# Expert weights behind all key scores: three engines in an order written by hand, and more of the first expert product ahead

## The chip, the core and the metric

The kernel runs on one core of a Trainium2 chip. A core has five engines, each with its own instruction queue that it works off in order: TensorE (PE in the rows, its weight loads PEld), VectorE (DVE), ScalarE (ACT), GpSimd (POOL) and SyncE (SP, which only issues DMAs). Sixteen DMA engines move data between the memories. The metric is the device time of one execution in microseconds (us).

## The reference, cut to what matters

One layer of a diffusion backbone on 512 tokens of width 1024: differential attention, a layer norm, and a PEER feed-forward with 16384 experts. The change is in the feed-forward alone.

```python
def peer_ffn(u, w_q, sub_keys, u_tab, v_tab):      # 8 heads, 128 keys per half, top 16
    ...
        q = (xb @ w_q).reshape(PEER_BLOCK, H, 2, PEER_QDIM // 2)
        s = jnp.einsum('thcd,ckd->thck', q, sub_keys).astype(F32)
        s1, i1 = lax.top_k(s[:, :, 0], KT)
        s2, i2 = lax.top_k(s[:, :, 1], KT)
        cand_s = (s1[..., :, None] + s2[..., None, :]).reshape(PEER_BLOCK, H, KT * KT)
        cand_i = (i1[..., :, None] * NK + i2[..., None, :]).reshape(PEER_BLOCK, H, KT * KT)
        top_s, pos = lax.top_k(cand_s, KT)
        idx = jnp.take_along_axis(cand_i, pos, axis=-1)
        g = jax.nn.softmax(top_s, axis=-1)
        act = jax.nn.gelu(jnp.einsum('thkd,td->thk', u_tab[idx], xb))
        return jnp.einsum('thk,thkd->td', (g * act).astype(xb.dtype), v_tab[idx])
```

## The kernel before, in words

After attention and its output projection the normed tokens lie on chip as two fp32r parts, `u2h` and `u2l`; a product in full accuracy is three matmuls (`mm3`, high by high, high by low, low by high). The 512 tokens are four tiles of 128. Tiles 0 to 2 (384 tokens) are done **densely** over all 16384 experts, tile 3 by **gathers** of the rows it chose: 128 rows of `peer_u` per token and 128 of `peer_v`.

- **Scores** (`scores`): 16 units, one for each head and half. A unit splits its query weights into two parts (ACT and POOL), makes a product of 24 matmuls of 512 columns, four key matmuls (eight records), and takes the top 16 of 128 for each tile on DVE (`top16`).
- **Choices** (`decide`): DVE finds the top 16 of 112 candidate sums, the two key indices of each and the softmax weights `gg`. It is called for half of the heads of one tile at a time, and calls for the first four heads are strewn between the later score units (`AT_K`).
- **Weights** (`gates`): for each dense tile eight steps of 16 tokens. DVE makes four one-hot arrays of 128x2048 fp16, PE multiplies them (32 matmuls of 128 columns), ACT copies four banks to `w`, and every second step SP writes 2 MB of `w` to DRAM (`gd`).
- **Up** (`up`): 128 tiles of 128 experts. SP loads the tile `ur`, ACT makes `uhi`, POOL `ulo`, PE does 24 matmuls of 384 columns, ACT the gelu into `at`. Tiles run ahead of the weights where `spilled` says so: 22 pairs (SPILL 21, and pair 0), whose `at` goes to DRAM (`ad`) and comes back (`ar`).
- **Down** (`down`): a loop over the 128 tiles `j`. ACT and DVE split the tile of `peer_v` (`vr`) into `vh` and `vl`, DVE multiplies weights by `at` (L951) and splits the product, PE does 18 matmuls of 512 columns into six banks. Up tiles that did not run ahead (84 of 128) come six tiles ahead in the same loop, and so do the gathers: POOL issues an indirect DMA (`fetch`, L897), DVE multiplies the row with the token (`gather`, L906, later L913). 14 of 256 gathers run ahead of the loop (`LATER`).

The order on each engine comes from a planner, which places instructions by its own costs and due times; `behind` adds an edge that only orders and carries no wait.

Of the kernel before, what the change touches and what calls it, by code (L numbers as in the profile page):

```python
# [9 lines left out]
F32 = mybir.dt.float32  # L10
FR = mybir.dt.float32r
# [20 lines left out]
SPILL = 21  # L32
LATER = {i: 1 for i in range(14, 42, 2)}
# [6 lines left out]
HG = 2  # L40
AT_K = {0: (3,), 2: (0,), 4: (1,), 6: (2,)}
# [17 lines left out]
def interleave(*streams):  # L59
# [20 lines left out]
    if late:  # L80
        late()


class Net:
# [35 lines left out]
    def mm3(self, out, pairs, first=True, last=True):  # L120

        nc = self.nc
        n = len(pairs)
        for i, (lh, ll, rh, rl) in enumerate(pairs):
            nc.tensor.matmul(out, lh, rh, start=first and i == 0, stop=False)  # L125
            nc.tensor.matmul(out, lh, rl, start=False, stop=False)  # L126
            nc.tensor.matmul(out, ll, rh, start=False, stop=last and i == n - 1)  # L127
# [534 lines left out]
    def peer(self):  # L662
# [3 lines left out]
        self.pp = es.enter_context(tc.tile_pool(name="pp", bufs=1, space=PSUM, reuse_waits="tile"))  # L666
        self.u2t = rp.tile([128, D], F32, name="u2t")
        nc.sync.dma_start(self.u2t, self.ud)
        self.i1f = rp.tile([128, NT, H * TK], F32, name="i1f")
        self.i2f = rp.tile([128, NT, H * TK], F32, name="i2f")  # L670
# [6 lines left out]
        self.GR, self.held, self.prepared = {}, (0, 0), None  # L677
        self.ad = self.dram.tile([64, 128, 2 * TD], F32, name="ad")
        self.gd = self.dram.tile([16, 128, TD // 32, 8, 32], F32, name="gd")
        self.ro = tc.alloc_tile_pool(name="ro", bufs=1, reuse_waits="tile")  # L680
        self.scores()
        self.ag = es.enter_context(tc.tile_pool(name="ag", bufs=1, side="right", reuse_waits="tile"))
        self.ug = tc.alloc_tile_pool(name="ug", bufs=1, side="right", reuse_waits="tile")
        self.row(self.g2, self.modc, 24, self.bank)
        with tc.tile_pool(name="gt", bufs=1, reuse_waits="tile") as gt:
            for t in range(DT):
# [20 lines left out]

    def bank(self):
        return self.pp.tile([128, 512], F32, name="v", bufs=6)

    def scores(self):
# [10 lines left out]
        with tc.tile_pool(name="qp", bufs=1, reuse_waits="tile") as qp:  # L722
# [9 lines left out]
            for k in range(1, 4):  # L732
                load(k)
            for k in range(2 * H):
                if k == 0:
                    q = self.q0
                else:
                    hi = qp.tile([128, KB, 128], FR, name="qhi", bufs=2)
                    lo = qp.tile([128, KB, 128], FR, name="qlo", bufs=2)
                    self.hi_lo(hi, lo, RAW[k], lo_engine=nc.gpsimd)  # L740
                    load(k + 3)
                    pq = self.bank()
                    self.mm3(pq, [(hi[:, kb], lo[:, kb], self.u2h[:, kb], self.u2l[:, kb]) for kb in range(KB)])
                    q = qp.tile([128, T], F32, name="q", bufs=2)
                    nc.scalar.activation(q, pq, AF.Copy)
# [363 lines left out]
```

## Time and profile before

| | us |
|---|---|
| median of 3 runs | 1810.55 |
| lowest and highest | 1802.44, 1813.66 |
| profiled execution | 1810.61 |
| its span, first to last instruction | 1808.8 |
| PE busy, DVE busy in the span | 1656.4, 1410.3 |
| ACT busy, POOL busy | 761.6, 909.8 |

The profiled execution took 1.8 us more than its span; the time is compared with 1810.61, which lies at the median. Matmuls are pipelined: their durations overlap, and what one costs is read from start to start.

### The profile page before, as it was taken

What the parts mean: (1) busy time and instruction counts of PE and PEld (TensorE: products, weight loads), DVE (VectorE), ACT (ScalarE), POOL (GpSimd) and SP (SyncE); (2) the same over time, 40 slices, a digit from 0 to 9 for tenths busy, and PEclk for the clock granted to TensorE, in tenths of its full rate; (3) what the DMA queues carried; (4) which work ended last, traced back from release to release, by engine and by line L of the source; (5) the groups of instructions that cost most, each with busy time, mean ns of one, the idle gap of its engine ahead of it and who ended that gap; (6) DMA issues with size and microseconds to landing.
All of it is one profiled execution on the core that took longest, in us unless ns stands there. A gap on an engine that the chain in (4) does not pass through costs nothing.

```text
span 1808.8 us, 24468 instructions
## 1 busy us (share of the span) xinstructions
PE 1656.4 (92%) x9041; PEld 1458.4 (81%) x9041; DVE 1410.3 (78%) x2571; ACT 761.6 (42%) x1150; POOL 909.8 (50%) x491
## 2 busy tenths in 40 slices
PE   7799899869899877787899999999999999999995
PEld 3678788857788777777888888988898989888884
DVE  6678787685459999999667877868777877778678
ACT  5465556442333336574643333333333333333332
POOL 3432323240343235435466767666666666667643
PEclk9899999979899989898999999999999999999997
DMA  7645645311532136667798888888888888988841
GB/s 307 174 141 152 175 123 151 100 58 36 202 110 91 46 99 234 224 222 237 240 394 332 319 333 335 318 311 339 332 338 308 308 326 317 341 335 313 308 177 58
DMA packets 119512, 418.87 MB, mean 232 GB/s; under 512 B 11488, under 2 KB 36576, under 8 KB 99808
## 3 DMA queue, kind: packets, MB, share of 16 engines
q1 hardware_dynamic: 61072, 188.17, 30.2%
q0 software_dynamic: 36864, 134.23, 19.9%
q10 hardware_dynamic: 21456, 94.91, 14.9%
q8 instruction: 71, 1.16, 0.3%
q14 instruction: 49, 0.40, 0.1%
HBM read 364.05 MB, written 38.54 MB: 223 GB/s over the span
## 4 chain that ended last, share of the span: by engine, by line
PE 50%; DVE 18%; issue 1%; DMA 1%; ACT 1%; POOL 0%; DVEq 0%; ACTq 0%; POOLq 0%
PE v L125 9%; PE v L127 9%; PE v L126 9%; PE a L125 7%; PE a L127 7%; PE a L126 7%; DVE oh L872 2%; DVE o L874 2%; DVE ol L873 1%; DVE idx L826 1%; DVE o L871 1%; DVE gr L906 1%; DVE pos L826 1%; DMA gq<-gd 1%; PE v L883 1%
## 5 line engine op out<-in xcount | busy, mean ns | idle before, releaser
L118 POOL TENSOR_TENSOR ulo<-ur,uhi 128x1024 fp32r<-128x1024 f32 x128 | 363.5, 2841 | 331.1 <-PE a L127 253.0
L125 PE MATMUL a<-u2h,uhi 128*128 128x384 f32 x1024 | 352.8, 344 | 8.3 <-ACT at L848 8.3
L127 PE MATMUL a<-u2h,ulo 128*128 128x384 f32 x1024 | 351.4, 343 | 0.5 <-POOL ulo L118 0.5
L126 PE MATMUL a<-u2l,uhi 128*128 128x384 f32 x1024 | 351.1, 343 | 0.0
L126 PE MATMUL v<-vl,wh 128*128 128x512 f32 x768 | 299.9, 391 | 4.0 <-DVE vl L118 4.0
L127 PE MATMUL v<-vh,wl 128*128 128x512 f32 x768 | 300.8, 392 | 1.8 <-DVE wl L118 1.8
L125 PE MATMUL v<-vh,wh 128*128 128x512 f32 x768 | 301.8, 394 | 0.7 <-ACT wh L115 0.7
L897 POOL DMA_INDIRECT gr<-in_peer_u_dram,eidx x128 | 176.4, 1378 | 86.7 <-DVE gr L906 60.2
L115 ACT ACTIVATE uhi<-ur 128x1024 fp32r<-128x1024 f32 x128 | 135.1, 1059 | 180.6 <-issue 110.0
L897 POOL DMA_INDIRECT gr<-in_peer_v_dram,eidx x128 | 162.6, 1271 | 92.8 <-DVE facc L913 60.8
L125 PEld LDWEIGHTS a<-u2h,uhi 128*128 128x128 f32 x1024 | 197.1, 192 | 12.8 <-ACT at L848 9.6
L126 PEld LDWEIGHTS a<-u2l,uhi 128*128 128x128 f32 x1024 | 197.3, 193 | 4.3 <-issue 0.4
L127 PEld LDWEIGHTS a<-u2h,ulo 128*128 128x128 f32 x1024 | 196.9, 192 | 1.5 <-POOL ulo L118 0.8
L118 DVE TENSOR_TENSOR vl<-vr,vh 128x1024 fp32r<-128x1024 f32 x128 | 164.8, 1288 | 32.9 <-ACT vh L115 32.9
L118 DVE TENSOR_TENSOR wl<-w,wh 128x384 fp32r<-128x384 f32 x128 | 76.2, 596 | 139.5 <-ACT wh L115 139.4
L913 DVE SCALAR_TENSOR_TENSOR facc<-gr,act,facc 128x1024 f32<-128x1024 f32 x127 | 171.0, 1346 | 4.3 <-DMA gr<-in_peer_v_dram,eidx 4.3
L115 ACT ACTIVATE vh<-vr 128x1024 fp32r<-128x1024 f32 x128 | 134.2, 1049 | 91.9 <-PE v L127 75.8
L127 PEld LDWEIGHTS v<-vh,wl 128*128 128x128 f32 x768 | 144.6, 188 | 34.6 <-DVE wl L118 2.3
L126 PEld LDWEIGHTS v<-vl,wh 128*128 128x128 f32 x768 | 144.8, 189 | 32.7 <-DVE vl L118 4.9
L125 PEld LDWEIGHTS v<-vh,wh 128*128 128x128 f32 x768 | 145.0, 189 | 28.5 <-ACT wh L115 1.4
L906 DVE SCALAR_TENSOR_TENSOR gr<-gr,u2t 128x1024 f32<-128x1024 f32 x128 | 165.4, 1309 | 2.5 <-DMA gr<-in_peer_u_dram,eidx 2.5
L115 ACT ACTIVATE wh<-w 128x384 fp32r<-128x384 f32 x128 | 66.5, 520 | 222.1 <-PE v L126 192.2
(268 smaller groups left out, 3250.1 us busy)
## 6 DMA issues: line engine op xcount, KB each, us to landing
ur<-in_u_t_dram SPq DMA_DIRECT2D x64, 1024.0 KB, 5.9
vr<-in_v_t_dram ACTq DMA_DIRECT2D x64, 1024.0 KB, 8.1
gq<-gd SPq DMA_DIRECT2D x16, 1536.0 KB, 11.2
gd<-w SPq DMA_DIRECT2D x12, 1920.0 KB, 8.0
adw<-in_ada_b_dram ACTq DMA_DIRECT2D x64, 256.0 KB, 3.3
wraw<-in_w_qkv_dram ACTq DMA_DIRECT2D x21, 512.0 KB, 4.2
ad<-at SPq DMA_DIRECT2D x22, 384.0 KB, 6.2
ar<-ad SPq DMA_DIRECT2D x22, 384.0 KB, 6.6
```

The costliest lines, as they stand in the source:

```text
L115: nc.scalar.activation(hi, src, AF.Copy)
L118: return (lo_engine or nc.vector).tensor_tensor(lo, src, hi.bitcast(F32), op=OP.subtract)
L125: nc.tensor.matmul(out, lh, rh, start=first and i == 0, stop=False)
L126: nc.tensor.matmul(out, lh, rl, start=False, stop=False)
L127: nc.tensor.matmul(out, ll, rh, start=False, stop=last and i == n - 1)
L826: nc.vector.max_index(idx[:, k], val[:, k], s)
L871: nc.vector.tensor_tensor(o2, io, wide(ii[:, 1]), op=OP.is_equal)
L872: nc.vector.tensor_tensor(oh, o2, wide(gh), op=OP.mult)
L874: nc.vector.tensor_tensor(o1, io, wide(ii[:, 0]), op=OP.is_equal)
L897: ins = nc.gpsimd.indirect_dma_start(out=self.GR[n], out_offset=None, in_=a["peer_v"] if n >= K else a["peer_u"], in_offset=bass.IndirectO ...
L906: ins = nc.vector.scalar_tensor_tensor(r, r, 1.0, self.u2t, op0=OP.mult, op1=OP.mult, accum_out=self.act[:, k:k + 1])
L913: ins = nc.vector.scalar_tensor_tensor(self.facc, r, self.act[:, k:k + 1], self.facc, op0=OP.mult, op1=OP.add)
```

## The change: what it does

- Instructions that go through the new class `Pinned` get an edge to the one before on their engine, so DVE (`V`), ACT (`A`) and PE (`T`) keep the order in which the program names them, from the first score to the last weight. POOL and SP are still placed by the planner.
- The scores run one product ahead of their key matmuls, with no choices and no up tiles between them, except one tile ahead of the last key matmuls.
- A choice covers all eight heads of a tile. The order is tile 3, 0, 1, then the weights of tile 0, then the choice of tile 2, then the weights of tiles 1 and 2.
- SPILL is 44: 45 pairs, 90 tiles, run ahead: 1 in the scores, 9, 9, 11 and 9 beside the four choices, 2 in each of 24 weight steps, 3 behind them. Each has its own load of 512 KB (four buffers) and is split up to three tiles ahead. Beside the weights and in the last 3, the low part is made by DVE and not by POOL.
- 64 gathers run ahead: 16 beside choices, 2 in each weight step; DVE uses a row three fetches later (`HOLD`). The token row that they are multiplied with lies in PSUM (`row2`) until the down loop.
- One-hots of the next step are made ahead of the matmuls of this one. PSUM: 4 banks for scores and weights, 2 for `row2`, 2 for up.

```diff
-SPILL = 21
-LATER = {i: 1 for i in range(14, 42, 2)}
+SPILL = 44
+WITH_CHOICE = {DT: (9, 0), 0: (9, 5), 1: (11, 6), 2: (9, 5)}
+WITH_GATES = (2, 2)
+HOLD = 3
...
+class Pinned:
+    def __getattr__(self, name):
+        def call(*args, **kwargs):
+            ins = getattr(self.engine, name)(*args, **kwargs)
+            self.net.pin(ins, ins)
+            return ins
+        return call
...
         self.scores()
+        self.choose(DT)
+        self.choose(0)
+        self.row(self.g2, self.modc, 24, self.bank, self.A, self.T)
         with tc.tile_pool(name="gt", bufs=1, reuse_waits="tile") as gt:
+            self.choose(1, lambda: self.turn(0))
+            self.split_gates(0)
+            self.onehot(0, 0)
             for t in range(DT):
-                self.gates(gt, t)
-                if t + 1 < DT:
-                    self.decide(t + 1, H - H // HG, H)
+                for n in range(128 // CH):
+                    if n == 4 and t + 1 < DT:
+                        self.turn(t + 1)
+                    if n + 1 < 128 // CH:
+                        self.onehot(t, n + 1)
+                    elif t + 1 < DT:
+                        self.split_gates(t + 1)
+                        self.onehot(t + 1, 0)
+                    self.ahead(*WITH_GATES, self.V)
+                    self.gates(t, n)
+                if t == 0:
+                    self.choose(2)
...
+        self.ahead(len(self.early) - self.done, 0, self.V)
...
+    def pin(self, begun, ins):
+        e = begun.ins.engine
+        if e in self.pinned:
+            self.behind(begun, self.pinned[e])
+        self.pinned[e] = ins
+
+    def ahead(self, n, rows=0, lo_engine=None):
+        for i in range(n):
+            while len(self.ready) < min(self.done + 3, len(self.early)):
+                j = self.early[len(self.ready)]
+                self.ready.append(self.split_up(j, self.A, lo_engine))
+            self.up(self.early[self.done], self.ready[self.done], self.A)
+            self.done += 1
+            new = rows * (i + 1) // n - rows * i // n
+            if new:
+                self.some(self.fetched + new, HOLD)
...
+            split(1)
             for k in range(2 * H):
+                split(k + 2)
+                if k + 1 < 2 * H:
+                    product(k + 1)
                 else:
+                    self.ahead(1)
                 ps = self.bank()
...
+    def split_up(self, j, act=None, lo_engine=None):
+        p, i, ug = j // 2, j % 2, self.ug
+        raw = ug.tile([128, KB, 128], F32, name="ur", bufs=4)
+        self.nc.sync.dma_start(raw.rearrange("p a b -> p (a b)"), self.a["u_t"][p, :, D * i:D * i + D])
+        hi = ug.tile([128, KB, 128], FR, name="uhi", bufs=3)
+        lo = ug.tile([128, KB, 128], FR, name="ulo", bufs=3)
+        (act or self.nc.scalar).activation(hi, raw, AF.Copy)
+        self.paced = (lo_engine or self.nc.gpsimd).tensor_tensor(lo, raw, hi.bitcast(F32), op=OP.subtract)
+        return hi, lo
...
         if n < K:
-            ins = nc.vector.scalar_tensor_tensor(r, r, 1.0, self.u2t, op0=OP.mult, op1=OP.mult, accum_out=self.act[:, k:k + 1])
+            ins = nc.vector.scalar_tensor_tensor(r, r, 1.0, self.row2, op0=OP.mult, op1=OP.mult, accum_out=self.act[:, k:k + 1])
```

## Rows read from the trace of the kernel before

**Rows 1.** Stretches of the span: start to mixing's end (479), scores, choices, weights, change to the down loop, loop, tail. Columns: us from and to, length, busy us and (instructions) of PE, PEld, DVE, ACT, POOL, granted PE clock (1.00 is the upper level), busy share of the DMA engines and GB/s.

```profile
479.00:492.00 13.00, 11.72 (x66) 10.67 (x65) 4.96 (x33) 5.82 (x7) 6.71 (x3) 1.00 0.57 207
492.00:545.00 53.00, 52.83 (x262) 44.24 (x262) 28.65 (x192) 16.85 (x25) 21.74 (x10) 1.00 0.36 116
545.00:677.00 132.00, 114.94 (x577) 102.66 (x577) 128.67 (x595) 46.65 (x65) 46.61 (x19) 0.94 0.23 77
677.00:905.00 228.00, 183.72 (x1425) 171.72 (x1425) 202.81 (x244) 139.41 (x164) 102.36 (x41) 0.90 0.70 231
905.00:927.00 22.00, 19.57 (x102) 18.93 (x101) 10.63 (x13) 9.94 (x14) 14.34 (x8) 0.92 1.02 423
927.00:1760.00 833.00, 833.00 (x4112) 744.48 (x4112) 650.11 (x733) 295.77 (x406) 552.70 (x324) 1.00 0.85 318
1760.00:1808.80 48.80, 30.51 (x115) 22.90 (x113) 41.04 (x61) 9.29 (x14) 20.31 (x9) 0.80 0.17 62
```

**Rows 2.** Waits of PE from 545 to 905 us: who waited for whom, us in total, times, longest.

```profile
PE v L882 <- DVE oh L872: 22.5, 11, 3.8
PE v L882 <- DVE o L874: 6.5, 2, 3.9
```

**Rows 3.** PE in order of time (start, us, line, tiles, shape, count): two up matmuls ten apart, two score products twenty apart, the eight key records of a unit and the product behind them, two weight matmuls ten apart, two down matmuls twelve apart, the last matmul of the loop.

```profile
835.00 0.34 PE L126 MATMUL a<-u2l,uhi 128*128 128x384 f32 x1
836.74 0.34 PE L127 MATMUL a<-u2h,ulo 128*128 128x384 f32 x1
...
581.09 0.40 PE L125 MATMUL v<-u2h,qhi 128*128 128x512 f32 x1
585.76 0.39 PE L127 MATMUL v<-u2h,qlo 128*128 128x512 f32 x1
...
604.39 1.16 PE L748 MATMUL v<-keys,q 128*128 128x128 f32 x8
605.31 0.48 PE L125 MATMUL v<-u2h,qhi 128*128 128x512 f32 x1
...
881.00 0.22 PE L882 MATMUL v<-oh,o 128*128 128x128 f16 x1
881.57 0.22 PE L883 MATMUL v<-ol,o 128*128 128x128 f16 x1
...
1100.20 0.39 PE L127 MATMUL v<-vh,wl 128*128 128x512 f32 x1
1102.92 0.39 PE L127 MATMUL v<-vh,wl 128*128 128x512 f32 x1
...
1765.41 0.39 PE L125 MATMUL v<-vh,wh 128*128 128x512 f32 x1
```

**Rows 4.** Start of the scores, in order of time: ACT's split of the first query weights, and PE's first matmul on the low part.

```profile
486.52 2.01 ACT L115 ACTIVATE qhi<-qraw 128x1024 fp32r<-128x1024 f32 x2
490.09 0.51 PE L127 MATMUL v<-u2h,qlo 128*128 128x512 f32 x1 [1.20 <-POOL qlo L118]
```

**Rows 5.** DVE around 487 us: first and last instruction of the top 16 of one score unit (four tiles), and, from the groups of 479 to 677 us (line, engine, operation, shapes, count, busy us, mean ns), the last sum of a half choice.

```profile
486.67 0.49 DVE L825 MAX8 val<-s 128x8 f32<-128x128 f32 x2 [4.85 <-ACT s L751]
491.15 0.29 DVE L826 FIND_INDEX8 idx<-val,s 128x8 uint32<-128x128 f32 x1
...
L811 DVE TENSOR_REDUCE i2f<-m 128x64 f32<-128x1024 bf16 x5 | 6.0, 1201 | 0.0
```

**Rows 6.** DVE and POOL beside each other in a weight step, in order of time.

```profile
826.06 1.90 POOL L897 DMA_INDIRECT gr<-in_peer_u_dram,eidx  x1 [1.37 <-DVE gr L906]
827.05 1.21 DVE L874 TENSOR_TENSOR o<-iota,ii 128x2048 f16<-128x2048 f16 x1
827.98 2.52 POOL L118 TENSOR_TENSOR ulo<-ur,uhi 128x1024 fp32r<-128x1024 f32 x1
828.19 3.40 DVE L872 TENSOR_TENSOR oh<-o,gh 128x2048 f16<-128x2048 f16 x1
831.50 1.21 DVE L873 TENSOR_TENSOR ol<-o,gl 128x2048 f16<-128x2048 f16 x1
```

**Rows 7.** Durations. Two rows by line (ns minimum/median/maximum, first and last start): a low part of 128x1024 on DVE, and a product with one input in PSUM, of half a row. Three rows of groups from 677 to 905 us: the gather's product, its indirect DMA and the low part on POOL.

```profile
L118 DVE TENSOR_TENSOR vl<-vr,vh x120: 1209/1221/3923, 935.5 to 1757.1; 128x1024 fp32r<-128x1024 f32 x120
L1024 DVE TENSOR_TENSOR gf<-v,g x6: 671/682/692, 1783.6 to 1798.9; 128x512 f32<-128x512 f32 x6
...
L906 DVE SCALAR_TENSOR_TENSOR gr<-gr,u2t 128x1024 f32<-128x1024 f32 x13 | 22.0, 1696 | 0.0
L897 POOL DMA_INDIRECT gr<-in_peer_u_dram,eidx x14 | 22.8, 1627 | 13.1 <-DVE gr L906 5.9 <-DVE eidx L765 3.5 <-ACT at L848 2.2
L118 POOL TENSOR_TENSOR ulo<-ur,uhi 128x1024 fp32r<-128x1024 f32 x27 | 79.6, 2948 | 112.3 <-PE a L127 97.7 <-ACT w L885 10.3 <-ACT uhi L115 4.1
```

**Rows 8.** From issue to landing: loads of `ur` over the whole span, gathers from 905 to 927 us.

```profile
DMA to landing us min/median/max: 4.7/5.9/14.9
DMA to landing us min/median/max: 11.7/14.3/16.3
```

**Rows 9.** Behind the last weights: ACT's last copies in order of time, the load of the first weights in the chain of work, the first down matmul.

```profile
889.84 3.85 ACT L885 ACTIVATE w<-v 128x512 f32<-128x512 f32 x4 [3.19 <-PE v L883]
901.32 14.76 DMA gq<-gd
927.01 0.39 PE L125 MATMUL v<-vh,wh 128*128 128x512 f32 x1
```

More of the change, by code (lines that the diff above doesn't have):

```diff
@@ L39 @@
 TM = 5
-HG = 2
-AT_K = {0: (3,), 2: (0,), 4: (1,), 6: (2,)}
 QT = 1
@@ L124, in mm3 @@
         for i, (lh, ll, rh, rl) in enumerate(pairs):
-            nc.tensor.matmul(out, lh, rh, start=first and i == 0, stop=False)
+            ins = nc.tensor.matmul(out, lh, rh, start=first and i == 0, stop=False)
+            begun = begun if i else ins
             nc.tensor.matmul(out, lh, rl, start=False, stop=False)
-            nc.tensor.matmul(out, ll, rh, start=False, stop=last and i == n - 1)
+            ins = nc.tensor.matmul(out, ll, rh, start=False, stop=last and i == n - 1)
+        return begun, ins
     def rsqrt_newton(self, y, v, tmp):
@@ L733, in scores, with split, product @@
                 load(k)
+            Q, S = {0: self.q0}, {}
+            def split(k):
+                if k < 2 * H:
+                    S[k] = [qp.tile([128, KB, 128], FR, name=x, bufs=2) for x in ("qhi", "qlo")]
+                    self.A.activation(S[k][0], RAW[k], AF.Copy)
+                    nc.gpsimd.tensor_tensor(S[k][1], RAW[k], S[k][0].bitcast(F32), op=OP.subtract)
+                    load(k + 3)
+            def product(k):
+                hi, lo = S[k]
+                pq = self.bank()
+                self.pin(*self.mm3(pq, [(hi[:, kb], lo[:, kb], self.u2h[:, kb], self.u2l[:, kb]) for kb in range(KB)]))
+                Q[k] = qp.tile([128, T], F32, name="q", bufs=2)
+                self.A.activation(Q[k], pq, AF.Copy)
@@ new lines, in up @@
+    def up(self, j, split=None, act=None):
+        p, i, ug = j // 2, j % 2, self.ug
+        if i == 0:
+            self.AT[p] = (ug if self.spilled(j) else self.gp).tile([128, 2, TD], F32, name="at", bufs=2)
+        hi, lo = split or self.split_up(j)
+        pa = self.pp.tile([128, 512], F32, name="a", bufs=2)
+        run = self.mm3(pa[:, :TD], [(hi[:, kb], lo[:, kb], self.u2h[:, kb, :TD], self.u2l[:, kb, :TD]) for kb in range(KB)])
+        if act:
+            self.pin(*run)
+        (act or self.nc.scalar).activation(self.AT[p][:, i], pa[:, :TD], AF.Gelu_apprx_tanh)
+        if self.spilled(j) and i == 1:
+            self.nc.sync.dma_start(self.ad[p], self.AT[p].rearrange("p j t -> p (j t)"))
@@ new lines, in onehot @@
+        wide = lambda x: x[:, CH * n:CH * n + CH].rearrange("p (a t) -> p a t", t=2)[:, :, None, :].to_broadcast(full)
+        o1, o2, oh, ol = [self.gt.tile(full, HF, name=x, bufs=y) for x, y in zip(("o1", "o2", "oh", "ol"), OB)]
+        self.V.tensor_tensor(o2, io, wide(ii[:, 1]), op=OP.is_equal)
+        self.V.tensor_tensor(oh, o2, wide(gh), op=OP.mult)
+        self.V.tensor_tensor(ol, o2, wide(gl), op=OP.mult)
+        self.V.tensor_tensor(o1, io, wide(ii[:, 0]), op=OP.is_equal)
+        self.O[t, n] = o1, oh, ol
@@ L915, in gather, with some @@
             self.behind(ins, self.prepared)
-    def some(self, n0, n1):
-        for n in range(n0, n1):
-            self.fetch(n)
-        for n in range(*self.held):
+        else:
+            self.pin(ins, ins)
+    def some(self, end, hold=0):
+        new = list(range(self.fetched, end))
+        for n in new:
+            self.fetch(n)
+        self.fetched = end
+        if hold:
+            self.held += new
+            use, self.held = self.held[:-hold], self.held[-hold:]
+        else:
+            use, self.held = self.held, new
+        for n in use:
             self.gather(n)
-        self.held = n0, n1
     def down(self):
@@ L928, in down @@
         self.gp = vp
-        acc = [[self.bank() for _ in range(2)] for _ in range(DT)]
+        ap = tc.alloc_tile_pool(name="acc", bufs=1, space=PSUM, reuse_waits="tile")
+        acc = [[ap.tile([128, 512], F32, name="v", bufs=6) for _ in range(2)] for _ in range(DT)]
         gq, vq, ready = {}, {}, {}
@@ L961, in down @@
         prepare(1)
-        n0 = self.held[1]
+        n0 = self.fetched
         at = lambda i: min(n0 + (256 - n0) * max(i, 0) // 116, 256)
```

227 lines of the change are left out of this document (116 added, 111 removed).

## The prediction

> **What bounds the kernel now.** I read the stretches first [rows 1]. From 927 to 1760 us PE is busy throughout at the upper clock level, with DVE at 78% and the DMA engines at 85%: the down loop is bound by PE, and an up tile taken out of it is worth its matmuls. From 545 to 905 us DVE is the busiest (128.7 of 132, 202.8 of 228 us), while PE has gaps and loses clock (0.94, 0.90). The waits say for whom: PE waits for the one-hots, 22.5 us and 6.5 us [rows 2].
>
> So the question is how much PE time is lost before the loop. A ledger of PE from 479 us to the loop's last matmul at 1765.7 us [rows 3], in costs from start to start at the upper clock: an up matmul 1.74/10 = 0.174 us, so a tile of 24 costs 4.16 (0.1733 each over a longer run); a score product matmul 4.67/20 = 0.2335, a product 5.6; the key matmuls of a unit 0.92; a weight matmul 0.057, a step of 32 1.84; a down matmul 2.72/12 = 0.227, 4.09 for one j of 18. By the program's counts: 128 x 4.16 = 532, 15 x 5.6 = 84, 16 x 0.92 = 15, 24 x 1.84 = 44, down (2304 less the 89 matmuls of the tail) x 0.227 = 503, row and transposes 1.5. Sum 1180 of 1287 us: **107 us are lost**, all but some 6 of them before 920 us. The program's PE work is the same after the change. The gain is 107 us less what the new order loses.
>
> **The change, part by part.** What each loses on PE:
>
> *Start, 479 to 488 us.* Before, up tiles fill PE until the first query weights are split (ACT 486.5, PE gets the low part at 490.1 [rows 4]). After, the first product stands ahead of everything on PE. ACT is free of the ups, so the split can come some 3 us earlier: PE idles from 479 to about 487.5 and comes out of that at the lower clock level, which doubles what the next few us of matmuls take. I take 11 (6 to 16).
>
> *Scores.* A unit costs PE 5.6 + 0.92 = 6.5 us, DVE 4.8 (486.7 to 491.4 [rows 5]), POOL under 3 [rows 7], ACT a split and two copies, some 3 [rows 4, 9]. PE sets the pace, and the key matmuls come a product late, so the copy between is hidden: loss 0. If that cover went, each unit would pay a copy of 128x512, about 1 us [rows 9], so the upper end is 15. They end near 487.5 + 15 x 6.5 = 585. The tile ahead of the last key matmuls waits for its first split, ACT 1.06 and POOL 2.4 to 2.9 [rows 7], behind a copy: loss 4. Last keys near 594.
>
> *Choices.* 479 to 677 us holds 162 us of DVE [rows 1]; 16 units take 77, and some 5.3 half choices (the last sum stands five times, the sixth is begun [rows 5]) the other 85: 16 us a half with its blocked operations, 32 a tile. PE gets 9 tiles = 37.4 us beside a choice, 45.8 beside that of tile 1; DVE adds 2, 6 and 5 gathers at 1.2 us: 32, 34, 39, 38 against 37, 37, 46, 37. POOL: nine low parts of 2.9 and five indirect DMAs of 1.6 [rows 7] are 35. ACT's Exp waits for DVE, and behind it on ACT stand the next tile's split and gelu, for which PE waits; but four tiles (16.6 us) come first, against some 12 us of DVE. Loss 4 (0 to 14).
>
> *Weight steps.* The largest term. PE: two tiles and a step, 8.32 + 1.84 = 10.16 us. DVE: four one-hots at 1.14 (827.05 to 828.19 [rows 6]), two low parts at 1.14 (1.21 less the overlap) and two gathers at 1.2 to 1.3: 9.3. The gather now has an input in PSUM; the nearest row, half a row with such an input, takes 0.68, so 1.3 for the whole [rows 7]. The 51 low parts cost DVE 58 us, but with them goes what POOL's low part does to DVE: a one-hot beside it takes 3.40 instead of 1.21 [rows 6]. ACT: four copies 3.85 [rows 9], two splits 2.0 [rows 4], two gelus below a copy's 1 each: under 8. The new order makes one-hots a step ahead, so PE waits for DVE no more, as long as DVE's 9.3 stays below 10.16. The DMA engines are the third candidate: by the shapes a step moves 1.05 MB of weights out, 1.05 MB of `ur`, 1.05 MB of gathers, 0.39 MB of `ad`: 3.54 MB. At 231/0.70 = 330 GB/s, the rate at full share in this stage [rows 1], that is 10.7 us; at 423 GB/s, seen from 905 to 927 us, 8.4. I take 10.9, as the nearer row is of this stage and no engine group runs at exactly 100%: loss 24 x 0.75 = 18 (0 to 48).
>
> *Change to the loop.* Before, 35 us pass from the last weight matmul (892) to the first down matmul (927.0), of which 14.8 are the load of `gq` [rows 9]; up tiles cover nearly all. After, `gd`, `gq`, DVE and ACT need 18 to 29 us; three tiles (12.5) and up to four not spilled, if the planner draws them forward (16.6), cover 12 to 29. Loss 6 (0 to 17).
>
> *Loop.* 38 up tiles remain, so one j costs PE 4.09 + 0.309 x 4.16 = 5.4 us instead of 6.8. DVE: vl 1.14, product and wl on 384 of its 1024 columns 0.45 each, 1.66 gathers at 1.25, 2.1: 4.1 and blocked time. Gathers still come at 0.31 per us, as 192 instead of 242 are left in a shorter loop. DMA: 0.524 (`vr`) + 0.162 + 0.197 (`gq`) + 0.138 (`ar`) + 0.87 (gathers) = 1.89 MB a j; at 318/0.85 = 374 GB/s 5.05 us, 94% of PE's time against 85% before. Loss 10 (3 to 40, if the rate is only 330). The 23 more pairs through DRAM are in these sums. On SP the loads of `ur` stand among stores that wait for ACT's gelus and copies, on POOL the gathers among low parts; the four raw buffers and three held rows cover such waits, and the third rival is the case where they don't.
>
> Sum: 11 + 0 + 4 + 4 + 18 + 6 + 10 = **53 us lost**, instead of 107. The tail is unchanged. 1810.6 - 54 = **1757 us**, 3.0% faster, against the profiled execution at 1810.61, which lies on the median of 1810.55.
>
> **Rivals.**
>
> *The DMA engines bound both stages.* At 330 GB/s the loop takes 1.89/0.33 = 5.7 us a j, 123 x 0.33 = 40 instead of 10, and some 8 more in the steps: loss 91, **1795**. For it: share 1.02 from 905 to 927, gathers landing in 14.3 us then [rows 8]. Against: that stretch moved 423 GB/s, and the loop before lost under 6 us at 85%.
>
> *DVE becomes the bound of the weight steps.* If an indirect DMA on POOL held up DVE as the low part does, two of 1.63 us a step [rows 7] would make DVE's step 12.6 us: 24 x 2.4 = 58 in place of 18, **1797**. Against it stands a row: the one-hot at 827.05 lies beside the indirect DMA of 826.06 to 827.96 and takes 1.21 [rows 6]. The Trainium skill, "SBUF — State Buffer", section "Who interferes with whom", says that a DVE instruction with two SBUF inputs contends with a GpSimd instruction that reads SBUF, and the second to issue blocks fully. The indirect DMA reads its row numbers from SBUF, so by that sentence this rival would hold; the row of the low part agrees with it, the row of the indirect DMA doesn't.
>
> *Slower: a late `ur` load at the head of ACT.* In the fixed order ACT waits for the tile's landing, and behind that wait stand the gelus and copies that free PE's banks. A raw buffer is loaded again when the tile four before it is split, 20 us ahead in a weight step; split and low part take 3.3. So a landing above 17 us sets the pace, at (landing + 3.3)/4 a tile. The kernel gets over 1% slower when the steps lose 90 us, 3.8 a step: 14 us a step, 7 a tile, landings of 24.7. At 26 us: 24 x 4.5 = 108, with 35 elsewhere 143 lost, **1846**. Measured are 5.9 in the median and 14.9 at most [rows 8].
>
> *The edges change nothing*, because the planner's order was no worse: then 46 tiles' 191 us go out of the loop and into stages that grow by as much, **1811**. Against it, PE's waits for one-hots in [rows 2], which an order with one-hots a step ahead removes.
>
> **How the numbers follow.** Forecast 0.67; DMA-bound 0.15; DVE-bound 0.06; late loads 0.08; no effect 0.04. The forecast's own ends, 20 lost with rates as from 905 to 927 and 90 with the upper ends of two terms, give 1724 to 1794. The range 1728 to 1806 cuts the lowest corner, takes in the DMA and DVE cases, and leaves the slower one and part of no effect out. Within 1% (1792.5 to 1828.7) is about what a measurement of this kernel can't tell from no change. Faster by more: the forecast nearly whole (0.64) and some 0.4 of the next two (0.09), 0.73. Slower: late loads and a little, 0.09. The rest, 0.18.
>
> **What would show it.** PE busy near 100% at the upper level from 490 to the loop's end, no waits on L872; scores in 6.5 us units, ending near 595; weight steps of 10.2 to 11 us; the first down matmul near 1045; 5.4 us a j; the DMA share near 0.95 in both. Wrong would be: a step of over 12 us, with PE waiting for `uhi` (late loads), for one-hots or `ulo` (DVE), or a loop of over 5.6 us a j with idle time on `vr`, `gq` or gathers.

## The result, and the profile after

The changed kernel takes **1749.95 us** (median; 1743.49 to 1754.3), the kernel before 1808.77 (1802.44 to 1813.66) beside it: a ratio of 0.9674, 95% interval [0.9629, 0.9719]. The forecast was 1757 with a range of 1728 to 1806. The profiled execution took 1748.19 us, 1746.4 of them its span. Two of the runs below had one execution each in a far slower state, which their times leave out. Below, the line numbers are those of the changed kernel: an up tile's split, gelu and matmuls are L94 on ACT, L141 to L144 on PE; `ur` is loaded on L928, gathers are issued on L1008 and used on L1017.

First the stretches, in the columns of [rows 1]: scores, choices, a part of the weight steps, change to the loop, loop, its end.

```profile
474.00:595.00 121.00, 109.99 (x532) 92.03 (x533) 95.62 (x488) 40.08 (x55) 44.39 (x19) 0.94 0.26 85
595.00:734.00 139.00, 132.71 (x771) 131.37 (x769) 133.84 (x308) 57.31 (x79) 91.19 (x42) 0.98 0.62 202
880.00:1000.00 120.00, 119.54 (x937) 117.46 (x935) 109.97 (x121) 76.71 (x95) 39.16 (x25) 1.00 1.00 356
1010.00:1051.00 41.00, 31.15 (x167) 29.00 (x165) 14.31 (x17) 16.43 (x21) 12.36 (x7) 0.88 0.93 349
1100.00:1600.00 500.00, 500.00 (x2365) 433.82 (x2364) 433.76 (x482) 177.33 (x242) 292.66 (x182) 1.00 0.93 349
1600.00:1690.00 90.00, 88.41 (x416) 75.74 (x414) 79.15 (x75) 30.65 (x43) 50.63 (x29) 1.00 0.87 315
```

PE now has its gaps ahead of the scores, around the first weight step and at the change to the loop. In between it is busy at the upper level, with DVE at 92% and the DMA engines at a share of 1.00 in the weight steps. All waits of PE from 590 to 1010 us, over a microsecond in total; the 29 us on one-hots of [rows 2] are down to 1.8:

```profile
PE a L144 <- DVE ulo L94: 3.4, 1, 3.4
PE v L94 <- DVE o L94: 1.8, 1, 1.8
PE a L144 <- POOL ulo L932: 1.4, 1, 1.4
PE a L141 <- ACT at L94: 1.2, 1, 1.2
```

PE where it stood still, in order of time (start, duration in us; in brackets the idle time before it and what ended it): the first product, the first weight step, the first down matmul, and the loop's last matmul with the one behind it.

```profile
480.29 0.80 PE L141 MATMUL v<-u2h,qhi 128*128 128x512 f32 x1 [6.53 <-ACT qhi L94]
...
729.63 0.23 PE L94 MATMUL v<-oh,o 128*128 128x128 f16 x1 [1.77 <-DVE o L94]
735.43 0.69 PE L144 MATMUL a<-u2h,ulo 128*128 128x384 f32 x1 [3.39 <-DVE ulo L94]
1040.65 0.79 PE L141 MATMUL v<-vh,wh 128*128 128x512 f32 x1 [9.85 <-ACT wh L131]
...
1689.21 0.39 PE L141 MATMUL v<-vh,wh 128*128 128x512 f32 x1
1696.41 0.79 PE L143 MATMUL v<-vl,wh 128*128 128x512 f32 x1 [6.82 <-DVE vl L134]
```

The prediction's ledger can be made for this trace, with the same cost of a matmul. From the end of mixing (473.76) to the loop's last matmul (1689.6) PE has 1215.8 us and 1167.4 of work, 12.3 less than before, because 143 matmuls of the loop now lie behind that point and not 89 (54 x 0.227 = 12.3). So **48.4 us are lost**, against 107 before and 53 forecast:

| lost on PE, us | forecast | after | what the trace shows |
|---|---|---|---|
| start | 11 | 10.1 | 6.5 and 1.2 idle, 2.3 by the lower clock level up to 486 |
| scores | 0 + 4 | 4.9 | units of 6.5; 1.7 and 1.8 idle on the first tile's split, 1.3 by the lower level behind it |
| choices | 4 | 6.1 | 1.2 and 1.4 idle at 617 to 620, 3.3 by the lower level behind them |
| weight steps | 18 | 9.6 | 7.1 around the first; the others mostly start every 10.24 us, 2.5 in all |
| change to the loop | 6 | 14.9 | 9.85 idle, 2.4 by the lower level up to 1046, 1.9 idle at 1060 on DVE's `wl` |
| loop | 10 | 2.8 | 0.8 from 1100 to 1600, 1.2 idle at 1619 |

The span is 62.4 us shorter: 58.6 less lost, 5.3 because mixing (the product that ends the part ahead of the scores) ends at 473.76 and not at 479.03, and the tail takes 1.5 longer, without its extra matmuls. The 5.3 are in no term of the forecast. 3.0 of them are there already when mixing's last transposes start (467.0 us, before 470.0), a point that lies between 465.0 and 471.9 in the eleven runs below in which, as in the changed kernel, the scores come first on PE: that part is luck. From there to the end of mixing it is 9.1 us before, and 6.6 to 7.0 in those runs and in the changed kernel. So the other 2.3 may belong to the change; there is one trace of before.

### The profile page after: what moved, and what is told of

Its sections match the earlier page's. It is cut to its first block, busy times and chain, and to the rows that moved or that the text cites. A ratio compares the mean times of both kernels' runs of the same rounds, so it can differ in the third digit from the quotient of the medians.

```text
span 1746.4 us, 24566 instructions
## 1 busy us (share of the span) xinstructions
PE 1625.9 (93%) x9041; PEld 1441.3 (83%) x9041; DVE 1448.4 (83%) x2539; ACT 753.5 (43%) x1140; POOL 784.8 (45%) x442
## 4 chain that ended last, share of the span: by engine, by line
PE 74%; DVE 10%; DMA 7%; issue 4%; ACT 3%; POOL 2%; SPq 0%; ACTq 0%; DVEq 0%; POOLq 0%
PE v L141 11%; PE v L144 11%; PE v L143 10%; PE a L144 9%; PE a L141 9%; PE a L143 9%; PE v L94 3%; DMA qs<-kh 2%; DMA adw<-in_ada_b_dram 2%; PE mp L218 1%; PE sc L405 1%; PE qkv L144 1%; DMA vr<-in_v_t_dram 1%; PE qkv L141 1%; PE qkv L143 1%
## 5 line engine op out<-in xcount | busy, mean ns | idle before, releaser
L144 PE MATMUL a<-u2h,ulo 128*128 128x384 f32 x1024 | 347.1, 339 | 6.6 <-DVE ulo L94 3.4
L141 PE MATMUL a<-u2h,uhi 128*128 128x384 f32 x1024 | 348.9, 341 | 2.9 <-ACT uhi L94 1.7
L143 PE MATMUL a<-u2l,uhi 128*128 128x384 f32 x1024 | 346.3, 338 | 0.0
L141 PE MATMUL v<-vh,wh 128*128 128x512 f32 x768 | 301.5, 393 | 10.3 <-ACT wh L131 10.3
L144 PE MATMUL v<-vh,wl 128*128 128x512 f32 x768 | 301.2, 393 | 3.7 <-DVE wl L134 1.9
L1008 POOL DMA_INDIRECT gr<-in_peer_u_dram,eidx x128 | 184.7, 1443 | 234.2 <-DVE gr L1017 219.5
L932 POOL TENSOR_TENSOR ulo<-ur,uhi 128x1024 fp32r<-128x1024 f32 x79 | 208.4, 2642 | 127.3 <-ACT uhi L94 70.6
L1008 POOL DMA_INDIRECT gr<-in_peer_v_dram,eidx x128 | 182.8, 1428 | 151.8 <-DVE facc L1024 128.9
L144 PEld LDWEIGHTS a<-u2h,ulo 128*128 128x128 f32 x1024 | 194.4, 190 | 7.6 <-POOL ulo L932 3.8
L141 PEld LDWEIGHTS a<-u2h,uhi 128*128 128x128 f32 x1024 | 194.3, 190 | 4.9 <-ACT uhi L94 1.9
L1024 DVE SCALAR_TENSOR_TENSOR facc<-gr,act,facc 128x1024 f32<-128x1024 f32 x127 | 183.9, 1448 | 7.6 <-DMA gr<-in_peer_v_dram,eidx 7.6
L141 PEld LDWEIGHTS v<-vh,wh 128*128 128x128 f32 x768 | 145.5, 190 | 39.9 <-ACT wh L131 11.0
L144 PEld LDWEIGHTS v<-vh,wl 128*128 128x128 f32 x768 | 145.4, 189 | 36.0 <-DVE wl L134 4.7
L94 ACT ACTIVATE at<-a 128x384 f32<-128x384 f32 x90 | 44.2, 491 | 190.1 <-PE a L144 101.1
L134 DVE TENSOR_TENSOR wl<-w,wh 128x384 fp32r<-128x384 f32 x128 | 94.8, 741 | 30.7 <-ACT wh L131 30.4
L134 POOL TENSOR_TENSOR wlo<-wraw,whi 128x1024 fp32r<-128x1024 f32 x24 | 61.0, 2546 | 82.0 <-ACT whi L131 61.4
```

The lines of the kernel that those rows point to most:

```text
L94: ins = getattr(self.engine, name)(*args, **kwargs)
L134: return (lo_engine or nc.vector).tensor_tensor(lo, src, hi.bitcast(F32), op=OP.subtract)
L141: ins = nc.tensor.matmul(out, lh, rh, start=first and i == 0, stop=False)
L144: ins = nc.tensor.matmul(out, ll, rh, start=False, stop=last and i == n - 1)
L932: self.paced = (lo_engine or self.nc.gpsimd).tensor_tensor(lo, raw, hi.bitcast(F32), op=OP.subtract)
L1008: ins = nc.gpsimd.indirect_dma_start(out=self.GR[n], out_offset=None, in_=a["peer_v"] if n >= K else a["peer_u"], in_offset=bass.IndirectO ...
```

## Experiments

Each edit is against the changed kernel. Times are set beside its repeat.

**The changed kernel again.** 

> The changed kernel once more, unaltered, as the mark for the runs beside it: 1750 us, a ratio of 0.967 to the kernel before, weight steps of 10.24 us from start to start, the first down matmul some 9.9 us late.

1751.4 us (1749.97 to 1756.7), ratio to before 0.9696 [0.9679, 0.9714]. From its trace come the landings, which the first one doesn't have. First `ur` from 880 to 1000 us, then gathers there (us from issue to landing, least, median, most). The median of `ur` is half as long again as over the whole span of before [rows 8], the longest is shorter.

```profile
DMA to landing us min/median/max: 4.9/8.9/12.7
DMA to landing us min/median/max: 6.3/9.0/11.8
```

**Seven tiles behind the last weight step.**

```diff
-SPILL = 44
+SPILL = 46
```

> SPILL 46 instead of 44: 94 tiles run ahead, so 7 instead of 3 stand behind the last weight step. If PE idles before the loop because it has nothing left to do while the first weights and rows of the second table are loaded, four tiles of 4.16 us cover the 9.9 us and the half clock behind them: 9 to 12 us faster than the changed kernel, some 1739 us. The rival is that the four tiles move the load and not only the matmuls: the first load of the loop starts when the last early tile lets go of its memory, so the gap comes back behind seven tiles, and the time stays at 1750.

1737.91 us (1736.95 to 1745.63), 0.9636 [0.9615, 0.9657]: 13.5 us faster than the repeat, and faster than both kernels. Where the load, the split and the product of the first down weights leave PE without work, there are tiles now. PE idles 2.1 us instead of 9.8 and keeps the upper clock level:

```profile
1036.60 0.44 PE L141 MATMUL a<-u2h,uhi 128*128 128x384 f32 x1 [2.09 <-ACT at L94]
...
1040.87 0.40 PE L141 MATMUL v<-vh,wh 128*128 128x512 f32 x1
```

The repeat idles 9.83 there, loses 2.9 by the lower clock level until 1054.6 and 1.6 on `wl` at 1068. By the ledger the change to the loop costs PE 14.7 us in the repeat and 4.7 here, 10 less, in the 9 to 12 that were expected; the medians lie 13.5 apart, the ratios 0.006, or 11 us. So that gap is worth about what PE loses in it, and more tiles spilled close it.

**Low parts of the weight steps back on POOL.**

```diff
-                    self.ahead(*WITH_GATES, self.V)
+                    self.ahead(*WITH_GATES)
```

> In the weight steps POOL makes the low parts again, as before the change. If POOL's low part holds up a DVE operation with two inputs in SBUF by 2.2 us, DVE's step goes from 9.3 less 2.3 plus 4.4 to 11.4 us and DVE sets the pace: 24 x 1.2 = 29 us slower than the changed kernel, 1779. If the low parts only weigh by their own time, DVE's step falls to 7.0, PE keeps 10.2 us, and the time stays at 1750.

1786.03 us (1783.85 to 1791.76), 0.9893 [0.987, 0.9916]: 35 us slower. The later steps take 11.7 us, and PE waits for one-hots (waits of PE, 860 to 1045 us). DVE and POOL beside each other in one step:

```profile
PE v L94 <- DVE o L94: 21.1, 15, 2.8
...
937.85 3.70 DVE L94 TENSOR_TENSOR o<-iota,ii 128x2048 f16<-128x2048 f16 x1
938.02 2.44 POOL L932 TENSOR_TENSOR ulo<-ur,uhi 128x1024 fp32r<-128x1024 f32 x1
940.61 1.76 POOL L1008 DMA_INDIRECT gr<-in_peer_u_dram,eidx  x1 [0.16 <-issue]
941.65 1.23 DVE L94 TENSOR_TENSOR oh<-o,gh 128x2048 f16<-128x2048 f16 x1
942.38 2.75 POOL L932 TENSOR_TENSOR ulo<-ur,uhi 128x1024 fp32r<-128x1024 f32 x1
942.79 3.42 DVE L94 TENSOR_TENSOR ol<-o,gl 128x2048 f16<-128x2048 f16 x1
```

A one-hot beside a low part takes 3.4 to 3.7 us, beside an indirect DMA 1.23, as in [rows 6]. Doing the low part on DVE costs it 1.14 and saves it 2.2 to 2.5. Sixteen steps of 1.46 more are 23 us; the gap ahead of the loop grows by 3 (12.65), and the stretch with the choice of tile 2 and the step behind it grow by 6, while the first step is 2 shorter; the two traces lie 28.9 us apart.

**The order left to the planner.**

```diff
-        if e in self.pinned:
+        if False:
```

> Everything of the change but the edges between neighbours on an engine: the planner may place DVE, ACT and PE as it likes. If the written order is what keeps PE fed, waits of PE for one-hots come back and 15 to 50 us of the gain go: 1765 to 1800. If the planner does as well by itself, as the rival of the prediction has it, 1750; and if the order in the program's text and the number of tiles do it alone, also 1750, with steps of 10.2 us.

1765.62 us (1758.38 to 1769.31), 0.9764 [0.9737, 0.9791]: 14 us slower by the medians, 12 by the ratios. So the edges are worth some 14 of the 54 us; the rest comes from what is done where. The weight steps stay at 10.24 us. More is lost beside the choices: PE's waits there (600 to 740 us), first without edges, then the largest three of the repeat (596 to 740 us).

```profile
PE a L141 <- ACT at L94: 23.8, 4, 9.4
...
PE v L94 <- DVE o L94: 5.1, 1, 5.1
PE a L144 <- POOL ulo L932: 2.9, 3, 1.4
PE a L141 <- ACT at L94: 2.7, 3, 1.6
```

But that isn't what makes this run longer. By the ledger it loses 54.4 us from the end of mixing to the loop's end, and the repeat 54.5: without edges the planner puts up tiles into the waits at the start and in the scores, which saves 14 us, and loses 13 beside the choices. The two traces lie 10.3 us apart, and mixing ends 10.6 later (486.3, the repeat 475.7). 4.7 of that is there already when mixing's first transposes start, ahead of any work on up tiles. 5.0 come from one wait of PE for DVE, 9.4 us instead of 4.4, where the planner put two low parts of up tiles on POOL. DVE beside them, on an instruction that takes 0.73 in the repeat:

```profile
472.11 5.09 POOL L932 TENSOR_TENSOR ulo<-ur,uhi 128x1024 fp32r<-128x1024 f32 x2 [46.65 <-DMA ur<-in_u_t_dram]
472.18 2.82 DVE L664 SCALAR_TENSOR_TENSOR u<-hp,lm,ga 128x512 f32<-128x512 f32 x1
```

**No gathers in the weight steps, and three instead of two.**

```diff
-WITH_GATES = (2, 2)
+WITH_GATES = (2, 0)
```

> The 48 gathers and products of the weight steps go to the down loop; all else stays. By PE setting the step, it stays at 10.24 us and the DMA share falls: 2.49 MB instead of 3.54 MB a step is a share near 0.72 in the stretch from 880 to 1000 us. The loop gets 240 gathers in 116 j instead of 192 (2.07 a j): 2.10 MB a j at 374 GB/s is 5.6 us against PE's 5.4, so the loop is bound by DMA and grows by 116 x 0.2 = 23 us: 1773 to 1785. By the rival, that DMA sets the step as well and PE only follows it, the step falls to what PE costs, 10.16: no more than 2 us come back. By the rival that the DMA rate in the loop has room (423 GB/s were seen), the loop stays at 5.4 us and the time within 5 us of 1751.

```diff
-WITH_GATES = (2, 2)
+WITH_GATES = (2, 3)
```

> Three gathers a weight step instead of two (94 ahead of the loop instead of 70). By the theory that the DMA engines are full in the step (share 1.00 to 1.04 at some 346 GB/s), 4.07 MB take 4.07/0.35 = 11.6 us: 24 x 1.4 = 33 us more, 1784, with PE waiting for ups or DVE for gathers. By the theory that DVE is next, its step grows from 9.3 by 1.21 to 10.5, or to 11.6 with the 0.93 us that it waits for a bank: 24 x 0.3 = 7 to 33 us. By the theory that neither binds (share 1.0 is queueing and not a limit), the step stays at 10.24 and the time near 1751. The DMA rate of the stretch tells the first from the second: at or below 350 GB/s with PE's wait on a landing, or 385 and above with PE's wait on a one-hot or a low part.

None: 1803.55 us (1792.68 to 1812.23), 0.9969 [0.994, 0.9998], 52 slower. Three: 1771.25 us (1768.4 to 1774.69), 0.9817 [0.9782, 0.9853], 20 slower. The stretch from 900 to 1000 us with none, two (the repeat) and three:

```profile
900.00:1000.00 100.00, 100.00 (x789) 98.41 (x788) 69.08 (x61) 65.10 (x79) 0.00 (x0) 1.00 0.76 247
900.00:1000.00 100.00, 100.00 (x788) 98.42 (x787) 92.05 (x103) 64.70 (x78) 32.90 (x20) 1.00 1.01 357
900.00:1000.00 100.00, 97.60 (x753) 96.00 (x752) 98.92 (x118) 62.69 (x78) 40.19 (x30) 1.00 1.04 389
```

The step is 10.24 us in all three. A share of 1.01 at 357 GB/s wasn't the limit: a third gather goes in at 389. It is PE that sets the step. That three are slower all the same comes from a few stalls, not from the rate: two steps are 8.4 and 2.9 us longer (6.8 on a low part that DVE makes late, DVE being 99% busy; 2.4 on ACT's copy), and the gap ahead of the loop is 11.7, in all 13 us; mixing ends 2.8 later, too. (64 and 88 rows are fetched ahead of the loop, not the 70 and 94 of the expectation.)

With none, the 48 gathers go into the loop, 2.07 a j instead of 1.66, and there the gathers do set the pace. The loop from 1100 to 1600 us, and what DVE and POOL wait for in it:

```profile
1100.00:1600.00 500.00, 473.59 (x2155) 399.12 (x2156) 449.42 (x535) 164.48 (x225) 318.49 (x203) 0.98 0.95 358
...
DVE gr L1017 <- DMA gr<-in_peer_u_dram,eidx: 29.8, 19, 2.9
DVE facc L1024 <- DMA gr<-in_peer_v_dram,eidx: 18.7, 13, 3.2
...
POOL gr L1008 <- DVE gr L1017: 84.1, 40, 4.1
POOL gr L1008 <- DVE facc L1024: 66.9, 59, 3.9
```

PE starts 2155 matmuls in 500 us instead of 2360, so a j takes 5.4 x 2360/2155 = 5.9 us, and 0.5 x 116 j are 58, near the 52 measured. The expectation took 374 GB/s from [rows 1] and so 5.6 us; the loop moves 358. That this is the limit of the transfers isn't shown. DVE's 449 us of work and 48.5 of waits for gathered rows fill 498 of the 500, and POOL waits 151 for DVE to hand back one of the five buffers before it can issue the next gather. A ring of five buffers with DVE near its limit would give the same rows; a run with more buffers, which would tell, wasn't made.

**A third of PE's work left out in 16 steps.**

```diff
+            if cross:
                 nc.tensor.matmul(out, lh, rl, start=False, stop=False)
...
+                       cross=not (55 <= self.done < 87))
```

> In up tiles 55 to 86, which lie in the 16 steps of weight tiles 1 and 2, the product of the high part of the weights with the low part of the tokens is left out (8 of 24 matmuls, so the activations of these tiles are less exact); all else is as after. PE's step falls from 10.16 to 7.4 us there. By the theory that the DMA engines are at their limit, as their share of 1.0 says, the step stays at 10.1 to 10.2 and the time at 1751. By the theory that DVE is next at 9.3, the step becomes 9.3 to 9.5: 16 x 0.8 = 13 us less, 1738. If neither holds and only PE bound it, the step becomes 8 us or less: 16 x 2.2 = 35 us less, 1716.

1762.39 us (1757.22 to 1765.66), 0.9761 [0.9726, 0.9796]: 11 us *slower* with 44 us less work (256 x 0.173), which none of the three theories expected. The edit also changed the order that the planner gave SP: in each two steps the four loads of `ur` now come in a row behind a store, where the repeat has them as three and one with stores between. SP, then ACT's next split (start, us, idle time before it):

```profile
916.98 4.75 SPq L949 DMA_DIRECT2D ad<-at  x1
921.81 3.27 SPq L929 DMA_DIRECT2D ur<-in_u_t_dram  x4
...
931.73 1.06 ACT L94 ACTIVATE uhi<-ur 128x1024 fp32r<-128x1024 f32 x1 [9.71 <-DMA ur<-in_u_t_dram]
```

SP is 4.8 us on the store, the loads follow, ACT stands 9.7 us until the first lands, PE runs dry and drops to the lower level (granted 0.50 from 933 to 936 us). Two steps take 23.5 us (964.6 to 988.1), where 15 were PE's part. It is the mechanism of the third rival, loads late at the head of ACT. In the repeat, with the other order, ACT waits for no load between 895 and 1035 us. Whether the new order alone makes the wait, or also the faster PE, one run doesn't separate. What DVE would have allowed stays unmeasured here; the next run tells that.

**One up tile a weight step.**

```diff
-SPILL = 44
+SPILL = 32
...
-WITH_GATES = (2, 2)
+WITH_GATES = (1, 2)
```

> One up tile instead of two beside each weight step (64 tiles ahead of the loop instead of 88; fewer pairs go through memory). PE's step falls to 4.16 + 1.84 = 6.0 us, DVE's from 9.3 to 8.2, the DMA engines move 2.3 MB, 6.6 us at 350 GB/s: by DVE as the next bound the step is 8.2 to 9.0. The 24 tiles, 100 us of PE, go into the loop, where PE is the bound: 62 tiles over 116 j. Steps give back 24 x (10.24 - 8.6) = 39: 1751 + 100 - 39 = 1812, as slow as before or a little slower. If the step falls to PE's 6.0, nothing is lost: 1751. If the loop has idle PE time to take the tiles, which the trace after denies (1 us lost in 600), less.

1802.09 us (1794.51 to 1806.08), 0.9984 [0.9962, 1.0005]: the gain is gone. Steps take 8.15 us (850.64, 858.79, 866.95), with DVE 103.6 of 105 us busy and PE waiting for it. That is the prediction's DVE sum less one low part, 9.3 - 1.14 = 8.2: with DVE's step known, PE's 10.24 is what binds at two tiles, with 0.9 in hand. Time: 24 x 4.16 = 100 into the loop, 24 x 2.09 = 50 back, 50 slower; 51 measured. So a tile beside a weight step costs half of what it saves in the loop.

**Two raw buffers instead of four.**

```diff
-        raw = ug.tile([128, KB, 128], F32, name="ur", bufs=4)
+        raw = ug.tile([128, KB, 128], F32, name="ur", bufs=2)
```

> Two raw buffers for the weights instead of four; nothing else. By the rule of the prediction's third rival, (landing + 3.3)/buffers a tile, with the landings of 9.3 us in the median that the repeat of the changed kernel shows between 880 and 1000 us: (9.3 + 3.3)/2 = 6.3 us a tile against PE's 5.12, a step of 12.6 instead of 10.24: 24 x 2.4 = 57 us, 1808, with PE waiting for the high part and ACT for the weights. With the landings of before, 5.9: 4.6 a tile, under PE's 5.12, nothing lost: 1751. If the order on the load queue (loads behind stores that wait for ACT) counts more than the landing, it is slower than 1808.

1784.39 us (1775.38 to 1786.35), 0.9863 [0.9818, 0.9907]: 33 slower, between the two. ACT's waits from 860 to 1010 us:

```profile
ACT uhi L94 <- DMA ur<-in_u_t_dram: 55.4, 18, 7.1
```

The later steps take 11.28 us on average, 5.64 a tile; by the rule (landing + 3.3)/2 that is a landing of 8.0, between 5.9 and 8.9 (the expectation's 9.3 is the repeat's median from 918 to 962 us). The semaphores of this run's trace put its own landings at 8.15 in the median, so the rule holds on average; step by step it doesn't, as eleven of the fifteen steps still take 10.24 to 10.27. Four buffers are what keeps the third rival away: with 8.9 us they allow (8.9 + 3.3)/4 = 3.1 a tile, against PE's 5.12.

**A gathered row held for one fetch, and the row's copy in SBUF.**

```diff
-HOLD = 3
+HOLD = 1
```

> A gathered row is used one fetch later instead of three, so DVE comes to it some half a weight step (5 us) after its issue instead of a step and a half (15 us). By the theory that the held rows cover late landings (9.0 us in the median), DVE waits some 4 us at each of 48 gathers of the weight steps, of which PE's slack on DVE (10.24 less 9.3 a step) takes a little: step 13 to 17 us, 24 x 3 to 7 = 70 to 160 us more, 1820 to 1910, if all of them are waited for; half of that if two gathers in a row share a wait. If landings fall under 5 us when nothing waits in the queue (4.9 is the least for weights), the time stays near 1751.

1761.82 us (1754.12 to 1765.09), 0.9737 [0.9694, 0.9779]. The steps stay at 10.24 us but for one of 13.42, and DVE waits for no gather in them. The expectation took 5 us from issue to use; by the order of the issues and the products in the trace there are at least 12.1 (19.4 with three held), against landings of 9.0 in the median and 11.8 at most. So one held row would have been cover enough there; three, as the prediction had it, are more than is needed. It is 10 us slower than the repeat by the medians, but the intervals of the ratios overlap. Of the 8.4 between the two traces 6.4 are lost beside the choices, where PE waits once for 10.1 us on a gelu; ACT stands 13.5 us in front of an Exp there, for DVE. Behind just this wait the prediction saw the next tile's split and gelu stand.

```diff
-            ins = nc.vector.scalar_tensor_tensor(r, r, 1.0, self.row2, ...)
+            ins = nc.vector.scalar_tensor_tensor(r, r, 1.0, self.u2t, ...)
```

> The products with gathered rows before the loop read the token's row from SBUF (the same values, already there) instead of the copy in PSUM. If two SBUF inputs make DVE share its port with POOL, the 22 products beside the choices, where POOL makes low parts, take up to 3.4 us instead of 1.21, and those of the weight steps, where POOL only issues gathers, stay at 1.21 to 1.3: 0 to 10 us slower, most of it hidden behind PE: 1751 to 1758. If issuing gathers held up DVE as well, the step would go from 9.3 to over 12 us: 1790. If PSUM has no part in it, 1751.

1754.98 us (1754.09 to 1763.75), 0.9738 [0.9685, 0.979], which can't be told from the repeat. The mechanism can be read off. First four rows of this run, beside low parts and beside an indirect DMA, then two of the repeat with the row in PSUM:

```profile
705.15 7.10 POOL L932 TENSOR_TENSOR ulo<-ur,uhi 128x1024 fp32r<-128x1024 f32 x3
706.53 6.81 DVE L1017 SCALAR_TENSOR_TENSOR gr<-gr,u2t 128x1024 f32<-128x1024 f32 x1
742.41 1.68 POOL L1008 DMA_INDIRECT gr<-in_peer_u_dram,eidx  x1 [9.93 <-DVE gr L1017]
743.19 1.22 DVE L1017 SCALAR_TENSOR_TENSOR gr<-gr,u2t 128x1024 f32<-128x1024 f32 x1
...
681.81 2.49 POOL L932 TENSOR_TENSOR ulo<-ur,uhi 128x1024 fp32r<-128x1024 f32 x1 [0.58 <-ACT uhi L94]
681.96 1.21 DVE L1017 SCALAR_TENSOR_TENSOR gr<-gr,row 128x1024 f32<-128x1024 f32 x1
```

With two inputs in SBUF, six products beside the choices meet low parts: three take 3.33, 3.89 and 6.81 us, some 10 us more in all, and three, which begin 0.6 us or more ahead of the low part, take 1.21 to 1.22. With one input in PSUM, all take 1.20 to 1.22 beside low parts. Beside an indirect DMA both take 1.22.

**Both gaps filled.**

```diff
-SPILL = 44
+SPILL = 47
...
-WITH_CHOICE = {DT: (9, 0), 0: (9, 5), 1: (11, 6), 2: (9, 5)}
+WITH_CHOICE = {DT: (9, 0), 0: (9, 5), 1: (13, 6), 2: (9, 5)}
```

> As the run with seven tiles behind the last weight step, and two more up tiles (8.3 us of PE) beside the choice of tile 1, where PE runs dry ahead of the first weight step: 5.1 us on a one-hot, 1.5 on a low part and 10.2 us at the lower clock level in the repeat of the changed kernel, 1.8 and 3.4 and 3.4 in the run with seven tiles. If DVE's choice is what ends there, and PE only waits for it, the tiles fill the wait and the loop loses them: 1738 less 5 to 9, so 1729 to 1733. If what the tiles need on DVE and POOL in that stretch (low parts) makes the choice end later by as much, it stays at 1738.

1737.32 us (1733.43 to 1743.26), 0.9615 [0.9583, 0.9648]: the same as with seven tiles alone, where 5 to 9 less was expected. PE's loss around the first weight step did fall, from 7.1 to 0.6 us. But 2.4 more are lost beside the choices, 1.9 at the start and in the scores and 0.5 in the tail. From the end of mixing on, the trace is only 2.3 us shorter than that with seven tiles, and mixing ended 3.8 us later; a gain of this size is within what differs from run to run.

## Why the prediction came out

The **diagnosis** was right: the loop is bound by PE, and what counts is the PE time lost ahead of it. 107 us became 48.4, where 53 were forecast. The terms were less good than their sum: three were off by 7 to 9 us each, two too high and one too low. That the sum came within 5 is in part luck.

- *Start, scores, choices* (forecast 19, after 21): right in size and place. Units of 6.5 us, POOL's first low part late, Exp and gelus on ACT.
- *Weight steps* (18, after 9.6). The step that failed is the price of the transfers: 3.54 MB at 330 GB/s, "no engine group runs at exactly 100%", hence 10.9 us; [rows 1] already had a stretch at 1.02. Three gathers a step went through at 389 GB/s, and most steps stayed at 10.24 us. The 231 GB/s at a share of 0.70 of [rows 1] told how long transfers lay in the queues, not how much would fit. PE's 10.16 was the right end of the range; measured is 10.24. DVE's 9.3 was right, too, as the run with one tile showed. But the first step, 7.1 of the 9.6, had no term: it waits for the last one-hots and a low part, behind the choice of tile 1.
- *Change to the loop* (6, after 14.9, inside the 0 to 17). What was too small is the chain, taken as 18 to 29 us: 29.7 pass from the last weight matmul (1010.97) to the first down matmul (1040.65). The cover was 19.8, in the middle of its 12 to 29: the three tiles, and 1.75 of the tiles not spilled, which the planner did draw forward. In order of time: the loads, ACT's split, DVE's low part and product, ACT's split of the product.

```profile
1019.40 0.37 ACTq L1056 DMA_DIRECT2D vr<-in_v_t_dram  x1
1019.52 1.26 SPq L1062 DMA_DIRECT2D gq<-gd  x1
1034.85 2.00 ACT L131 ACTIVATE vh<-vr 128x1024 fp32r<-128x1024 f32 x2 [10.80 <-DMA vr<-in_v_t_dram]
1035.94 1.23 DVE L134 TENSOR_TENSOR vl<-vr,vh 128x1024 fp32r<-128x1024 f32 x1 [20.30 <-ACT vh L131]
1037.08 0.55 DVE L1071 TENSOR_TENSOR w<-gq,ar 128x384 f32<-128x384 f32 x1
1040.09 0.51 ACT L131 ACTIVATE wh<-w 128x384 fp32r<-128x384 f32 x1
```

  `vr` is issued 8.4 us after the last weight matmul, behind the tiles' splits and gelus on ACT, and needs 15 us to land, with the DMA engines at a share of 1.00 (365 GB/s); splits and products take 6 more. The forecast took the load of `gq` for what comes last, as in [rows 9]. `vr` is as late: in the repeat both are issued within 0.1 us, and these are the first `gq` and the first `vr` from issue to landing.

```profile
DMA to landing us min/median/max: 15.2/15.2/15.2
DMA to landing us min/median/max: 15.3/15.3/15.3
```

  The run with seven tiles behind the last step shows what more cover is worth.
- *Loop* (10, after 2.8). 349 GB/s for 1.89 MB is 5.4 us, PE's own time. The end of PE's lead isn't far: at 2.07 gathers a j the loop stalls, whatever it is that binds there. Here the low end of 3 was right. The DMA-bound rival was wrong in both stages by its rate of 330: 356 and 349 GB/s went through while PE was busy.
- The *DVE rival* falls with the rows of DVE beside indirect DMAs, 1.22 us with both inputs in SBUF. For low parts the sentence of the Trainium skill, "SBUF — State Buffer", section "Who interferes with whom", that the second to issue blocks fully, agrees with 6.81 us behind the rest of one low part and two more, and the one that an instruction with a single SBUF input doesn't contend agrees with 1.21 beside one.
- The *slower rival* stayed away, with landings of at most 12.7 us against the 17 it needs. Its mechanism is real: two raw buffers cost 33 us, and the run with less work on PE and the loads in a row on SP lost 11, with ACT waiting for them.
- The rival that the *edges change nothing* was wrong in its time, 1811, but not far off on the edges alone: from the end of mixing on, the planner's order loses as much as the written one (54.4 and 54.5), and makes the steps in 10.24, too. It treated order and placement as one; most of the gain is placement (low parts on DVE 35, two tiles a step 51, gathers ahead 52, each taken away alone, so that they don't add up).

## What to carry to other kernels

Make a ledger of the engine that bounds the kernel, work against span from stage to stage. Its sum came out here in part because errors of both signs cancelled, but each gap that remains in it names its own repair (here 13.5 us for four more tiles ahead of the loop). Look for slack in every stage before moving work there: two gathers a step were free in the weight steps, where the step is 10.24 us with and without them, and cost 52 us in the loop. And follow the first item of the next stage through every queue that it crosses: the loads for the loop were issued 8.4 us after the last weights, behind splits and gelus on ACT's queue, and needed 15 more to land.

## What the runs showed of the hardware

The busy share of the DMA engines is no measure of what room is left: 0.76, 1.01 and 1.04 stood beside 247, 357 and 389 GB/s in one and the same stretch, so a third gather a step still went through at a share of 1.01. The Trainium skill, "Perfetto Trace Analysis", section "Identifying the Most-Contended Engine", advises to judge the DMA engines by the utilization of the memory and not by occupancy, and then to find what really binds; the three figures agree with the first half. For the second there is the loop with more gathers, which stalled at 358 GB/s and 0.95: whether the transfers or the ring of five row buffers held it there stays open.

A DVE instruction that starts behind POOL's can wait for more than one: 6.81 us behind three low parts that followed each other without a gap. With one operand in PSUM no such wait was seen (1.20 to 1.22 beside low parts).
